# A build-time scheduler that books a port shared by VectorE and GpSimd, with costs taken from a trace: hybrid decoder trunk, 2 layers, 1 core

## The chip, the cores and the metric

The kernel runs on one core of a Trainium2 chip. The time is the device time of one execution in microseconds (us). An execution under the profiler gives the traces; its own time is listed beside its span.

The engines are called as the profile calls them: PE (TensorE, with PEld for its weight loads), DVE (VectorE), ACT (ScalarE), POOL (GpSimd) and SP (SyncE, whose queue issues the DMAs). SBUF is the on-chip memory, PSUM the accumulators that PE writes.

## The reference

Two layers over x of 512 tokens by 1024 channels, all in float32. Each layer is a mixer and a feed-forward part, with an RMS norm ahead of each and one behind it, added to x. In short:

```
for l in range(2):
    h = rmsnorm(x, pre_mix_norm[l])
    proj = h @ w_in[l]                    # k, v, q, z: 4 heads of 128; bq, bk, bv: 8 heads of 64; a, b
    q, k, v = silu(causal_conv4(q, k, v)) # q, k then l2-normalised
    o_a = gated_delta_rule(q, k, v, g, beta)      # chunked; triangular solve in each chunk
    o_a = rmsnorm(o_a, dn_out_norm) * silu(z)
    o_b = dilated_attention(rope(bq), rope(bk), bv)   # three window/dilation pairs
    x = x + rmsnorm(concat(o_a, o_b) @ w_out[l], post_mix_norm[l])
    h = rmsnorm(x, pre_ffn_norm[l])
    u = causal_conv3(h @ ffn_up[l]) + bias
    x = x + rmsnorm((gelu(gate) * val) @ ffn_down[l], post_ffn_norm[l])
```

## The kernel before, in words

Channels lie on the 128 partitions and the 512 tokens along a row, so x is 8 tiles of 128x512. A float32 product with a weight is made of three products in the type fp32r: the high part of the weight with the high and with the low part of x, and the low part of the weight with the high part of x (`mm3`, L305; `mmk`, L310). Each weight comes in units of 128x1024. `loader` issues the DMA of a unit into one of two `raw` buffers. `splitter` has ACT copy it to fp32r (`whi`), then subtracts that from `raw` to get `wlo`: VectorE in one operation of 128x1024, or GpSimd in four of 128x256. Four pairs of buffers (`HL`) hold split units; a new copy to `whi` waits until PE has finished the unit that had the buffer before.

The order of every engine's instructions is made at build time by a small scheduler, `_Sched` (L46). It has a clock `t`, which each matmul moves on (`mm`, L132), and for VectorE, ACT and GpSimd a time from which each is free. The parts of the computation are generators (`gates`, `decays`, `conv`, `silu`, `inverse`, `attention`, `score`, `splitter` and so on). Each emits instructions, books their cost with `op` (L76) and yields until the time at which it may go on; the job with the best priority whose time has come goes next. So a changed cost changes no instruction's work, but can change the order of emission, and that is the program's order on each engine. It can also change which engine does a step where the scheduler may choose: the `wlo` split (VectorE or GpSimd), and the scaling of an attention row by its reciprocal sum (ACT or GpSimd, `score`). On the chip each engine then runs its list in order and waits for what it needs.

What the change's steps touch, in the mixer:

- The units come in the order k, v (4 heads each), bq, bk, bv (4 units each), q, z, then 8 of the out-projection. The convolution of k and v (`conv`, L779) is `A<-psg,rs` on VectorE, one step on ACT and three on VectorE (`kT<-A,vv,kT`, 128x509 to 128x511; `vb<-A,vv,vb` for v).
- `gates` (L712) works out the decay gate `dn_g` on VectorE in small steps, and then has PE multiply it with a triangle: `pso<-dn_g,cc`. `silu` (L803) of k loads ACT's silu table, runs kT (128x2048) and loads the exp table again.
- `decays` (L765): four times `pso<-cc,dn_g` on PE, `edec<-pso,dn_gc` on VectorE (L771), two steps on ACT. PSUM tag `o` has one buffer, so the next product waits for the `edec` before it.
- `k_head` (L819): transposes of kT (`pss<-cc,kT`), a square and its sum, and `kd<-pss,dn_kds`; tag `s` has three buffers.
- `inverse` (L860) solves the triangles, with two round trips through DRAM, and `attention` (L1180) makes 8 heads of 4 scores: `psg<-bT,..` on PE, the masked minimum `nm` on VectorE, exp and its sum `den` on ACT, a reciprocal on VectorE, the scaling of `A` or `B` on ACT or GpSimd, transposes on PE (`psg<-cc,B`), a copy `pt` on ACT and its low part on VectorE, and the product with `vh`. The last of it and z (`zt`) become `hx`, which the out-projection multiplies.

The cost lines before the change, for VectorE's and GpSimd's two-operand step (`tt`):

```
n = out_.free_size()
return sc.op(eng, 0.07 + n * 1.05e-3 if eng == "dve" else 0.18 + n * 2.07e-3, after)
```

Of the kernel before, what the change touches and what calls it, by code (L numbers as in the profile page):

```python
# [43 lines left out]
class _Sched:  # L44
# [69 lines left out]
def kernel(ctx: ExitStack, tc: tile.TileContext, xT, w_ab, w_cm, w_tm, w_o, w_up, w_dn,  # L114
# [14 lines left out]
    sc = _Sched()  # L129


    def mm(ps, lhsT, rhs, start, stop):  # L132
        n = rhs.free_size()
        if rhs.dtype == F32R:
            sc.t += n / 2400.0 if n >= 256 else 0.107
        else:
            sc.t += max(0.214 if lhsT.free_size() > 64 else 0.11, n / 600.0)
        pe.matmul(ps, lhsT, rhs, start=start, stop=stop)  # L138

    def transposes(dst, srcs):  # L140
        for i, s in enumerate(srcs):
            sc.t += 0.109
            pe.transpose(dst[:, i * P:(i + 1) * P], s, ident)

# [5 lines left out]
    def tt(out_, a, b, op, after=0.0, eng="dve"):  # L150
        (nc.vector if eng == "dve" else nc.gpsimd).tensor_tensor(out_, a, b, op=op)  # L151
        n = out_.free_size()
        return sc.op(eng, 0.07 + n * 1.05e-3 if eng == "dve" else 0.18 + n * 2.07e-3, after)

    def ts(out_, a, s1, s2, op0, op1=None, after=0.0, eng="dve"):
        e = nc.vector if eng == "dve" else nc.gpsimd
        if op1 is None:
            e.tensor_scalar(out_, a, s1, None, op0=op0)  # L158
# [3 lines left out]
        return sc.op(eng, 0.07 + n * 1.0e-3 if eng == "dve" else 0.17 + n * 8.5e-4, after)

    def stt(out_, a, s, b, op0, op1, after=0.0):
        nc.vector.scalar_tensor_tensor(out_, a, s, b, op0=op0, op1=op1)  # L165
        return sc.op("dve", 0.07 + out_.free_size() * 1.05e-3, after)
# [1394 lines left out]
```

## Time and profile before

| what | value |
|---|---|
| median of 3 runs | 1411.7 us (1410.64 to 1413.77) |
| profiled execution: its time | 1419.57 us |
| profiled execution: its span | 1417.5 us |
| mean granted PE clock | 0.981 |
| matmuls on PE in the profile | 7174 |
| table loads on ACT | 19, 24.4 us in all |

A row of the page gives an engine's busy time, its share of the span and its count. A row of the windows gives a stretch, its length, then busy time and count of PE, PEld, DVE, ACT and POOL, the granted clock, the DMA share and GB/s. A row of the timeline gives the start, the length, the engine, the kernel's line, the operation, out<-in, the shape and how many in a row, and in brackets the idle time of the engine ahead of it with what ended it; rows of one kind in a row are drawn together. Float32 matmuls stand in the records as two each, so x8 is four products.

### The profile page before, as it was taken

What the parts mean: (1) busy time and instruction counts of PE and PEld (TensorE: products, weight loads), DVE (VectorE), ACT (ScalarE), POOL (GpSimd) and SP (SyncE); (2) the same over time, 40 slices, a digit from 0 to 9 for tenths busy, and PEclk for the clock granted to TensorE, in tenths of its full rate; (3) what the DMA queues carried; (4) which work ended last, traced back from release to release, by engine and by line L of the source; (5) the groups of instructions that cost most, each with busy time, mean ns of one, the idle gap of its engine ahead of it and who ended that gap; (6) DMA issues with size and microseconds to landing.
All of it is one profiled execution on the core that took longest, in us unless ns stands there. A gap on an engine that the chain in (4) does not pass through costs nothing. (4 is left out here: it accounts for less than half of the span.)

```text
span 1417.5 us, 19282 instructions
## 1 busy us (share of the span) xinstructions
PE 1375.4 (97%) x7174; PEld 1145.6 (81%) x7174; DVE 861.9 (61%) x1512; ACT 618.0 (44%) x998; POOL 719.2 (51%) x778
## 2 busy tenths in 40 slices
PE   9999999998999999999989999999989999999996
PEld 5878777887888888888878887788888888888886
DVE  4774477847677777421569544778478777773213
ACT  5553466635544344232345433665345444433220
POOL 5455266414577777334173541663155777772441
PEclk9999999999999999999999987999999999999998
DMA  5233111052233232333332330110512333333331
GB/s 200 75 94 87 61 46 45 16 164 75 72 92 104 90 105 89 94 98 99 98 131 68 116 88 16 45 46 23 171 60 79 100 97 98 94 96 88 106 93 60
DMA packets 48701, 123.17 MB, mean 87 GB/s; under 512 B 15584, under 2 KB 18400, under 8 KB 48608
## 3 DMA queue, kind: packets, MB, share of 16 engines
q1 hardware_dynamic: 48608, 121.95, 27.8%
q8 instruction: 57, 0.93, 0.3%
q14 instruction: 36, 0.29, 0.1%
HBM read 115.11 MB, written 6.82 MB: 86 GB/s over the span
## 5 line engine op out<-in xcount | busy, mean ns | idle before, releaser
L151 POOL TENSOR_TENSOR wlo<-raw,whi 128x256 fp32r<-128x256 f32 x560 | 500.8, 925 | 357.9 <-ACT whi L147 343.9
L138 PE MATMUL psg<-hx,whi 128*128 128x512 f32 (+1 forms) x2080 | 631.9, 387 | 2.4 <-DVE hx L151 2.4
L138 PEld LDWEIGHTS psg<-hx,whi 128*128 128x128 f32 x2080 | 379.9, 189 | 76.1 <-DVE hx L151 3.4
L138 PE MATMUL psg<-hx,wlo 128*128 128x512 f32 (+1 forms) x1040 | 396.5, 381 | 0.0
L147 ACT ACTIVATE whi<-raw 128x1024 fp32r<-128x1024 f32 (+1 forms) x200 | 209.0, 1045 | 428.1 <-PE psg L138 367.5
L138 PEld LDWEIGHTS psg<-hx,wlo 128*128 128x128 f32 x1040 | 196.3, 189 | 38.2
L165 DVE SCALAR_TENSOR_TENSOR B<-A,vv,B 128x510 f32<-128x510 f32 (+1 forms) x176 | 199.4, 1135 | 39.3 <-ACT B L147 36.1
L138 PE MATMUL psg<-hid,whi 128*128 128x512 f32 (+1 forms) x744 | 213.1, 371 | 0.0
L138 PEld LDWEIGHTS psg<-hid,whi 128*128 128x128 f32 x744 | 135.6, 188 | 24.1
L151 DVE TENSOR_TENSOR wlo<-raw,whi 128x1024 fp32r<-128x1024 f32 (+1 forms) x58 | 73.7, 1273 | 133.6 <-ACT whi L147 133.6
L138 PE MATMUL psg<-hid,wlo 128*128 128x512 f32 (+1 forms) x372 | 137.9, 371 | 0.0
L138 PE MATMUL psg<-whi,hx 128*128 128x512 f32 x384 | 125.0, 407 | 0.7 <-DVE A L151 0.7
L151 POOL TENSOR_TENSOR acc<-acc,sq 128x256 f32<-128x256 f32 (+1 forms) x65 | 65.8, 1013 | 104.4 <-ACT sq L147 102.5
L151 DVE TENSOR_TENSOR A<-psg,rs 128x512 f32<-128x512 f32 x100 | 68.7, 689 | 40.8 <-PE psg L138 38.8
L138 PEld LDWEIGHTS psg<-whi,hx 128*128 128x128 f32 x384 | 70.1, 191 | 14.6 <-DVE A L151 1.5
L138 PEld LDWEIGHTS psg<-hid,wlo 128*128 128x128 f32 x372 | 70.0, 188 | 12.0
L138 PE MATMUL psg<-wlo,hx 128*128 128x512 f32 x192 | 76.2, 397 | 0.0
L147 ACT ACTIVATE B<-A,vv 128x512 f32<-128x512 f32 x88 | 70.2, 802 | 2.6 <-DVE A L151 2.6
L147 ACT ACTIVATE C<-B 128x512 f32<-128x512 f32 x44 | 27.7, 630 | 86.2 <-DVE B L165 86.1
L151 DVE TENSOR_TENSOR hid<-C,hid 128x512 fp32r<-128x512 f32 x44 | 36.3, 826 | 28.3 <-ACT hid L147 28.3
L158 POOL TENSOR_SCALAR B<-B,den 128x512 f32<-128x512 f32 (+1 forms) x30 | 41.0, 1368 | 23.8 <-DVE den L177 13.7
L138 PE MATMUL pss<-hx,whome 128*128 128x256 f32 x288 | 42.6, 305 | 5.2 <-DVE hx L165 4.6
(239 smaller groups left out, 1704.8 us busy)
## 6 DMA issues: line engine op xcount, KB each, us to landing
raw<-in_w_up_dram SPq DMA_DIRECT2D x88, 512.0 KB, 3.5
raw<-in_w_cm_dram SPq DMA_DIRECT2D x32, 512.0 KB, 3.6
raw<-in_w_dn_dram SPq DMA_DIRECT2D x32, 512.0 KB, 3.5
raw<-in_w_tm_dram SPq DMA_DIRECT2D x24, 512.0 KB, 3.5
raw<-in_w_o_dram SPq DMA_DIRECT2D x16, 512.0 KB, 3.5
raw<-in_w_dn_dram SPq DMA_DIRECT2D x16, 384.0 KB, 3.1
xt<-in_xT_dram SPq DMA_DIRECT2D x7, 512.0 KB, 7.0
scr_a<-am SPq DMA_DIRECT2D x8, 256.0 KB, 2.7
```

The source lines that it names most:

```text
L138: pe.matmul(ps, lhsT, rhs, start=start, stop=stop)
L147: nc.scalar.activation(out_, in_, func, **kw)
L151: (nc.vector if eng == "dve" else nc.gpsimd).tensor_tensor(out_, a, b, op=op)
L158: e.tensor_scalar(out_, a, s1, None, op0=op0)
L165: nc.vector.scalar_tensor_tensor(out_, a, s, b, op0=op0, op1=op1)
```

## The change

`_Sched` gets a time `port` from which the way to SBUF that VectorE and GpSimd share is free. An operation booked with `port=True` starts no earlier than that and moves it to its own end. VectorE's `tt`, `ts` and `stt` book it unless an operand lies in PSUM (`in_psum`); GpSimd's always do. The costs of these steps and the pitch of the products change: a product of n columns in fp32r from n/2400 to n/2400 + 0.0134, GpSimd's `ts` from 0.17 + n x 8.5e-4 to 0.17 + n x 2.7e-3, and so on. `tiled` moves the clock on by 0.095 whenever the stationary tile goes between up to 64 and more rows or columns. The same matmuls are made, and the same buffers are used; what changes is the order on each engine and the engine of some steps.

```
--- before.py
+++ after.py
@@ -55,6 +55,7 @@
         self.slots = {}
         self.flags = {}
         self.chain = False
+        self.port = 0.0
 
     def spawn(self, gen, prio=1, at=0.0):
         self.jobs.append([prio, self.n, max(self.t, at), gen])
@@ -73,8 +74,12 @@
             except StopIteration:
                 self.jobs.remove(job)
 
-    def op(self, eng, cost, after=0.0):
+    def op(self, eng, cost, after=0.0, port=False):
+
         start = max(self.free[eng], self.t, after)
+        if port:
+            start = max(start, self.port)
+            self.port = start + cost
         self.free[eng] = start + cost
         return start + cost + 0.2
 
@@ -129,16 +134,29 @@
     sc = _Sched()
 
 
+    shape = [None]
+
+    def tiled(lhsT):
+        now = (lhsT.shape[0] <= 64, lhsT.free_size() <= 64)
+        if now != shape[0]:
+            shape[0] = now
+            sc.t += 0.095
+
     def mm(ps, lhsT, rhs, start, stop):
         n = rhs.free_size()
+        tiled(lhsT)
         if rhs.dtype == F32R:
-            sc.t += n / 2400.0 if n >= 256 else 0.107
+            sc.t += n / 2400.0 + 0.0134 if n >= 256 else 0.107
         else:
-            sc.t += max(0.214 if lhsT.free_size() > 64 else 0.11, n / 600.0)
+            sc.t += max(0.22 if lhsT.free_size() > 64 else 0.117, n / 600.0 + 0.01)
         pe.matmul(ps, lhsT, rhs, start=start, stop=stop)
+
+    def in_psum(*aps):
+        return any(a.tensor.name.startswith("ps") for a in aps)
 
     def transposes(dst, srcs):
         for i, s in enumerate(srcs):
+            tiled(s)
             sc.t += 0.109
             pe.transpose(dst[:, i * P:(i + 1) * P], s, ident)
 
@@ -150,7 +168,9 @@
     def tt(out_, a, b, op, after=0.0, eng="dve"):
         (nc.vector if eng == "dve" else nc.gpsimd).tensor_tensor(out_, a, b, op=op)
         n = out_.free_size()
-        return sc.op(eng, 0.07 + n * 1.05e-3 if eng == "dve" else 0.18 + n * 2.07e-3, after)
+        if eng == "dve":
+            return sc.op(eng, 0.09 + n * 1.06e-3, after, not in_psum(a, b))
+        return sc.op(eng, 0.18 + n * 2.2e-3, after, True)
 
     def ts(out_, a, s1, s2, op0, op1=None, after=0.0, eng="dve"):
         e = nc.vector if eng == "dve" else nc.gpsimd
@@ -159,11 +179,13 @@
         else:
             e.tensor_scalar(out_, a, s1, s2, op0=op0, op1=op1)
         n = out_.free_size()
-        return sc.op(eng, 0.07 + n * 1.0e-3 if eng == "dve" else 0.17 + n * 8.5e-4, after)
+        if eng == "dve":
+            return sc.op(eng, 0.09 + n * 1.05e-3, after, not in_psum(a))
+        return sc.op(eng, 0.17 + n * 2.7e-3, after, True)
 
     def stt(out_, a, s, b, op0, op1, after=0.0):
         nc.vector.scalar_tensor_tensor(out_, a, s, b, op0=op0, op1=op1)
-        return sc.op("dve", 0.07 + out_.free_size() * 1.05e-3, after)
+        return sc.op("dve", 0.09 + out_.free_size() * 1.13e-3, after, not in_psum(a, b))
 
     def red(out_, a, after=0.0):
         nc.vector.tensor_reduce(out_, a, axis=AX.X, op=ALU.add)
```

Where the program differs, at the two places that the prediction speaks of. Names carry a tile's number, which differs between the kernels; lines of the kernel after are 18 to 22 higher.

The first place is layer 0, where the decays start. PE before: the second and the third decay product (`pso<-cc,dn_g`), with three of kT's four transposes between them. Fifteen fp32r products follow the third one, the first six in these rows, and then the fourth.

```order
L138 MATMUL pso_582<-cc_80,dn_g_305 128x128 x4
L143 MATMUL pss_587<-cc_80,kT_292 128x128 x4
L143 MATMUL pss_595<-cc_80,kT_292 128x128 x4
L143 MATMUL pss_602<-cc_80,kT_292 128x128 x4
L138 MATMUL pso_609<-cc_80,dn_g_305 128x128 x4
L138 MATMUL psg_536<-hx1_105,whi_372 128x512 x2
L138 MATMUL psg_536<-hx1_105,wlo_373 128x512
L138 MATMUL psg_624<-whi_450,hx0_104 128x512 x2
L138 MATMUL psg_624<-wlo_451,hx0_104 128x512
```

PE after, from the first of kT's transposes to the first products of bq behind them:

```order
L161 MATMUL pss_595<-cc_80,kT_289 128x128 x4
L161 MATMUL pss_602<-cc_80,kT_289 128x128 x4
L161 MATMUL pss_611<-cc_80,kT_289 128x128 x4
L152 MATMUL pso_618<-cc_80,dn_g_302 128x128 x4
L152 MATMUL pso_642<-cc_80,dn_g_302 128x128 x4
L161 MATMUL pss_650<-cc_80,kT_289 128x128 x4
L152 MATMUL psg_664<-whi_424,hx0_104 128x512 x2
L152 MATMUL psg_664<-wlo_425,hx0_104 128x512
```

The second decay product (`pso_618`) has moved behind three transposes, and the third (`pso_642`) follows it directly; the fourth transpose of kT comes after both.

VectorE there, before: `edec` of the first three decay products and the six steps of v's convolution.

```order
L151 TENSOR_TENSOR edec_294<-pso_561,dn_gc_309 128x512
L151 TENSOR_TENSOR edec_294<-pso_582,dn_gc_309 128x512
L165 SCALAR_TENSOR_TENSOR vb_293<-A_534,vv_89,vb_293 128x509
L165 SCALAR_TENSOR_TENSOR vb_293<-A_534,vv_89,vb_293 128x510
L165 SCALAR_TENSOR_TENSOR vb_293<-A_534,vv_89,vb_293 128x511
L165 SCALAR_TENSOR_TENSOR vb_293<-A_559,vv_89,vb_293 128x509
L165 SCALAR_TENSOR_TENSOR vb_293<-A_559,vv_89,vb_293 128x510
L165 SCALAR_TENSOR_TENSOR vb_293<-A_559,vv_89,vb_293 128x511
L151 TENSOR_TENSOR edec_294<-pso_609,dn_gc_309 128x512
```

And after:

```order
L169 TENSOR_TENSOR A_568<-psg_420,rs_103 128x512
L169 TENSOR_TENSOR wlo_563<-raw_536,whi_562 128x1024
L169 TENSOR_TENSOR edec_291<-pso_570,dn_gc_306 128x512
L187 SCALAR_TENSOR_TENSOR vb_290<-A_550,vv_89,vb_290 128x509
L187 SCALAR_TENSOR_TENSOR vb_290<-A_550,vv_89,vb_290 128x510
L187 SCALAR_TENSOR_TENSOR vb_290<-A_550,vv_89,vb_290 128x511
L187 SCALAR_TENSOR_TENSOR vb_290<-A_568,vv_89,vb_290 128x509
L187 SCALAR_TENSOR_TENSOR vb_290<-A_568,vv_89,vb_290 128x510
L187 SCALAR_TENSOR_TENSOR vb_290<-A_568,vv_89,vb_290 128x511
L169 TENSOR_TENSOR edec_291<-pso_618,dn_gc_306 128x512
```

`edec` of the second product has moved behind the six steps, and the split of bq's last unit (`wlo_563`), which GpSimd did, stands ahead of the first.

ACT there, before: from the last convolution step of k through silu of kT between its two table loads to the copy of bq's last unit, `whi_628`.

```order
L147 ACTIVATE kT_292<-A_496,vv_89 128x512
L147 ACTIVATE whi_540<-raw_486 128x1024
L219 ACT_TABLE_LOAD
L147 ACTIVATE kT_292<-kT_292 128x2048
L219 ACT_TABLE_LOAD
L147 ACTIVATE vb_293<-A_534,vv_89 128x512
L147 ACTIVATE vb_293<-A_559,vv_89 128x512
L147 ACTIVATE edec_294<-edec_294 128x512 x2
L147 ACTIVATE sq_592<-pss_587 128x512
L147 ACTIVATE sq_600<-pss_595 128x512
L147 ACTIVATE edec_294<-edec_294 128x512 x2
L147 ACTIVATE whi_628<-raw_532 128x1024
```

And after, where that copy is `whi_562`:

```order
L165 ACTIVATE kT_289<-A_502,vv_89 128x512
L165 ACTIVATE whi_547<-raw_525 128x1024
L165 ACTIVATE whi_562<-raw_536 128x1024
L241 ACT_TABLE_LOAD
L165 ACTIVATE kT_289<-kT_289 128x2048
L241 ACT_TABLE_LOAD
L165 ACTIVATE vb_290<-A_550,vv_89 128x512
L165 ACTIVATE vb_290<-A_568,vv_89 128x512
```

The copy has moved from behind the decays' steps to ahead of the silu and its table load.

The second place is the end of attention in layer 0 (layer 1 reads the same). ACT before: `A` and `B` with `den` are exps of scores, the last one `B_2586`; `zt` 128x1536 is silu of three heads of z.

```order
L147 ACTIVATE A_2485,den_2584<-A_2485,nm_2549 128x384
L147 ACTIVATE sq_2592<-vb_293 128x512
L147 ACTIVATE bT0_298<-pso_2519 64x512
L147 ACTIVATE vb_293<-pss_2608,vv_89 128x4x128
L147 ACTIVATE B_2586,den_2617<-B_2586,nm_2589 128x512
L219 ACT_TABLE_LOAD
L147 ACTIVATE pt0_1479<-psg_2625 128x2x128
L147 ACTIVATE pt1h_1480<-psg_2641 128x3x128
L147 ACTIVATE zt_2166<-zt_2166 128x1536
```

And after, where the last exp is `B_2598`:

```order
L165 ACTIVATE pt1h_1305<-psg_2588 128x4x128
L165 ACTIVATE A_2567,den_2596<-A_2567,nm_2570 128x384
L241 ACT_TABLE_LOAD
L165 ACTIVATE zt_2072<-zt_2072 128x1536
L165 ACTIVATE vb_290<-pss_2613,vv_89 128x4x128
L165 ACTIVATE pt0_1304<-psg_2619 128x128
L165 ACTIVATE B_2526<-B_2526,den_2573 128x256
L241 ACT_TABLE_LOAD
L165 ACTIVATE B_2598,den_2624<-B_2598,nm_2601 128x512
L241 ACT_TABLE_LOAD
L165 ACTIVATE bT0_295<-pso_2542 64x512
```

The silu of z with its table load has moved ahead of the last exp, which has a load on both sides now, and a scaling (`B_2526<-B_2526,den`) that GpSimd did has come to ACT.

VectorE there, before, around the last reciprocal (`den_2617`):

```order
L151 TENSOR_TENSOR bT0_298<-pso_2519,bT0_298 64x512
L151 TENSOR_TENSOR zt_2166<-psg_2317,rs_103 128x512
L177 RECIPROCAL den_2617<-den_2617 128x1
L151 TENSOR_TENSOR vb_293<-vb_293,dn_rq_314 128x4x128
L151 TENSOR_TENSOR pt0_1479<-psg_2625,pt0_1479 128x2x128
L151 TENSOR_TENSOR pt1l_1481<-psg_2641,pt1h_1480 128x3x128
L151 TENSOR_TENSOR zt_2166<-zt_2166,vb_293 128x512 x3
L151 TENSOR_TENSOR pt1l_1481<-psg_2672,pt1h_1480 128x4x128
L151 TENSOR_TENSOR zt_2166<-psg_2630,rs_103 128x512
```

And after, around `den_2624`:

```order
L169 TENSOR_TENSOR pt0_1304<-psg_2619,pt0_1304 128x128
L169 TENSOR_TENSOR zt_2072<-zt_2072,vb_290 128x512 x3
L169 TENSOR_TENSOR zt_2072<-psg_2575,rs_103 128x512
L199 RECIPROCAL den_2624<-den_2624 128x1
L169 TENSOR_TENSOR bT0_295<-pso_2542,bT0_295 64x512
L169 TENSOR_TENSOR pt0_1304<-psg_2656,pt0_1304 128x2x128
L169 TENSOR_TENSOR pt1l_1306<-psg_2663,pt1h_1305 128x3x128
L169 TENSOR_TENSOR hx0_2668<-zt_2072,hx0_2668 128x512
```

The product of z with the recurrence's output (`vb`) and the last head's `zt<-psg` have moved ahead of the last reciprocal.

More of the change, by code (lines that the diff above doesn't have):

```diff
@@ L57, in __init__ @@
         self.chain = False
+        self.port = 0.0
     def spawn(self, gen, prio=1, at=0.0):
@@ L74, in run, with op @@
                 self.jobs.remove(job)
-    def op(self, eng, cost, after=0.0):
+    def op(self, eng, cost, after=0.0, port=False):
         start = max(self.free[eng], self.t, after)
+        if port:
+            start = max(start, self.port)
+            self.port = start + cost
         self.free[eng] = start + cost
@@ L129, with tiled, in_psum @@
     sc = _Sched()
+    shape = [None]
+    def tiled(lhsT):
+        now = (lhsT.shape[0] <= 64, lhsT.free_size() <= 64)
+        if now != shape[0]:
+            shape[0] = now
+            sc.t += 0.095
     def mm(ps, lhsT, rhs, start, stop):
         n = rhs.free_size()
+        tiled(lhsT)
         if rhs.dtype == F32R:
-            sc.t += n / 2400.0 if n >= 256 else 0.107
+            sc.t += n / 2400.0 + 0.0134 if n >= 256 else 0.107
         else:
-            sc.t += max(0.214 if lhsT.free_size() > 64 else 0.11, n / 600.0)
+            sc.t += max(0.22 if lhsT.free_size() > 64 else 0.117, n / 600.0 + 0.01)
         pe.matmul(ps, lhsT, rhs, start=start, stop=stop)
+    def in_psum(*aps):
+        return any(a.tensor.name.startswith("ps") for a in aps)
     def transposes(dst, srcs):
         for i, s in enumerate(srcs):
+            tiled(s)
             sc.t += 0.109
@@ L152, in tt @@
         n = out_.free_size()
-        return sc.op(eng, 0.07 + n * 1.05e-3 if eng == "dve" else 0.18 + n * 2.07e-3, after)
+        if eng == "dve":
+            return sc.op(eng, 0.09 + n * 1.06e-3, after, not in_psum(a, b))
+        return sc.op(eng, 0.18 + n * 2.2e-3, after, True)
     def ts(out_, a, s1, s2, op0, op1=None, after=0.0, eng="dve"):
@@ L161, in ts @@
         n = out_.free_size()
[L162 removed]
+        if eng == "dve":
+            return sc.op(eng, 0.09 + n * 1.05e-3, after, not in_psum(a))
+        return sc.op(eng, 0.17 + n * 2.7e-3, after, True)
     def stt(out_, a, s, b, op0, op1, after=0.0):
         nc.vector.scalar_tensor_tensor(out_, a, s, b, op0=op0, op1=op1)
[L166 removed]
+        return sc.op("dve", 0.09 + out_.free_size() * 1.13e-3, after, not in_psum(a, b))
     def red(out_, a, after=0.0):
```

## The prediction

> **What bounds the kernel now.** I read the page first, then the windows, the waits of TensorE (PE) and the timelines of the places that wait. The first block is the page; the second is busy time by stretch (PE, PEld, DVE, ACT, POOL, granted clock, DMA share).
>
> ```profile
> span 1417.5 us, 19282 instructions
> PE 1375.4 (97%) x7174; PEld 1145.6 (81%) x7174; DVE 861.9 (61%) x1512; ACT 618.0 (44%) x998; POOL 719.2 (51%) x778
> ```
> ```profile
> 70.00:105.00 35.00, 32.89 (x179) 27.15 (x178) 27.92 (x67) 20.26 (x27) 19.79 (x26) 1.00 0.32 95
> 735.00:770.00 35.00, 32.84 (x162) 27.35 (x162) 30.27 (x53) 20.20 (x31) 16.04 (x20) 0.95 0.25 81
> 1085.00:1400.00 315.00, 315.00 (x1444) 263.08 (x1443) 169.45 (x175) 113.16 (x144) 180.00 (x191) 1.00 0.30 91
> ```
> ```profile
> 143.18:176.05 32.87, 32.81 (x268) 25.55 (x268) 15.66 (x59) 14.52 (x33) 8.84 (x11) 1.00 0.18 62
> 839.14:882.44 43.30, 43.08 (x268) 33.80 (x268) 16.16 (x59) 14.53 (x33) 8.81 (x11) 0.72 0.15 49
> ```
>
> PE is the bound. In the feed-forward stretch (1085 to 1400) it is busy without a gap, and the order gives the weight splits there to the same engines as before, so nothing is won or lost there. What can change lies in the two mixers (layer 0 up to about 280, layer 1 from 735 to 985) and the hand-overs between stages. In two of their stretches, 70:105 and 735:770, VectorE is busy for 28 and 30 of 35 us and PE has gaps: what VectorE is given there, PE feels. The last two rows are the same 268 matmuls in layer 0 and layer 1: 10.4 us more at a clock of 0.72. The profiled execution took 1419.57 us (span 1417.5 and 2.1 around it), 7.9 above the median of 1411.7; I put that down to such stretches and add my sum to the median, clock left out. This kernel's runs tell about 0.2% (2.8 us) from no change.
>
> The waits of PE (total, times, longest):
>
> ```profile
> PE psg L138 <- DVE hx L151: 2.4, 2, 1.2
> PE pso L138 <- DVE dn_g L165: 1.9, 1, 1.9
> PE pss L143 <- DVE A L151: 1.9, 4, 0.5
> PE psg L138 <- DVE nm L1208: 1.7, 2, 0.9
> ```
>
> In the mixers all are small, 8 us together. A new order can win at most these, and it loses wherever it puts a dependent product nearer to its source than the chain on the other engines is long. So I went through the order of both kernels for the places where that distance changes.
>
> **Layer 0, the decays: the largest term.** The four decay products `pso<-cc,dn_g` share one PSUM buffer, so each waits for VectorE's `edec` of the one before. Before, in PE, ACT and DVE:
>
> ```profile
> 60.58 1.05 PE L138 MATMUL pso<-cc,dn_g 128*128 128x128 f32 x8
> ...
> 62.86 0.62 PE L138 MATMUL psg<-hx,whi 128*128 128x512 f32 x2
> ...
> 63.55 1.05 PE L138 MATMUL pso<-cc,dn_g 128*128 128x128 f32 x8
> 64.44 1.47 PE L143 MATMUL pss<-cc,kT 128*128 128x128 f32 x12
> 65.75 1.06 PE L138 MATMUL pso<-cc,dn_g 128*128 128x128 f32 x8
> 66.56 0.70 PE L138 MATMUL psg<-hx,whi 128*128 128x512 f32 x2
> ...
> 70.83 1.16 PE L138 MATMUL pso<-cc,dn_g 128*128 128x128 f32 x8 [0.58 <-DVE edec L151]
> ...
> 75.24 0.74 PE L138 MATMUL psg<-whi,hx 128*128 128x512 f32 x2 [0.33 <-DVE A L151]
> ```
> ```profile
> 61.63 1.92 ACT L147 ACTIVATE kT<-kT 128x2048 f32<-128x2048 f32 x1 [1.30 <-DVE kT L165]
> 63.57 1.28 ACT L219 ACT_TABLE_LOAD   x1
> 64.86 1.33 ACT L147 ACTIVATE vb<-A,vv 128x512 f32<-128x512 f32 x2
> ...
> 69.45 1.04 ACT L147 ACTIVATE whi<-raw 128x1024 fp32r<-128x1024 f32 x1
> ```
> ```profile
> 65.62 4.55 DVE L165 SCALAR_TENSOR_TENSOR vb<-A,vv,vb 128x509 f32<-128x509 f32 x6 [0.29 <-ACT vb L147]
> 70.09 0.69 DVE L151 TENSOR_TENSOR edec<-pso,dn_gc 128x512 f32<-128x512 f32 x1
> ...
> 71.92 0.68 DVE L151 TENSOR_TENSOR kd<-pss,dn_kds 128x512 f32<-128x512 f32 x1
> ...
> 75.11 0.68 DVE L151 TENSOR_TENSOR edec<-pso,dn_gc 128x512 f32<-128x512 f32 x1
> ```
>
> A group of three fp32r products takes 0.69 (62.86 to 63.55), one 0.23. The new order does three things. First, 12 more of them stand ahead of the gates' product, and as many as before between it and the decays, so the first decay product moves to 60.58 + 12 x 0.23 = 63.34; nothing else is late by then. Second, ACT copies bq's last weight unit (`whi_562`) ahead of the silu of kT; that copy needs the buffer of the last v unit, which PE finishes only at 63.3 (before, this copy stood behind: the row at 69.45). So ACT: copy to 64.4, table load to 65.7, silu 1.92 to 67.6, load to 68.9, convolution of v from 68.9. VectorE's six steps start 0.76 behind (64.86 to 65.62): 69.7. Third, `edec` of the second product now stands behind these six, and the third product follows the second on PE with nothing between. `edec` starts 4.47 after the six start (65.62 to 70.09): 74.15, done 74.85. PE is there at 63.34 + 0.81 (a decay product, 65.75 to 66.56) + 2.76 (12 products) + 1.31 (kT's transposes, 64.44 to 65.75) + 0.81 = 69.0, and waits 5.9; before, it waited 0.58 once. Queued behind the waiting copy on ACT are the two loads, the silu and all of v's convolutions; VectorE's split of the same unit waits too (64.4 to 65.7), and the first `edec` behind it is done by 66.4, before PE needs it at 68.2. GpSimd waits for nothing there. Behind it, kd ends 1.82 after `edec` (70.78 to 72.60): 76.7; from there one reduction, kd, two A and `edec` make 3.2 (72.60 to 75.79 before, same five and a 0.2): done 79.9; the fourth product ends at 80.8. The same work was behind PE at 75.24 before: **+5.55**. Below: were the copy out of the silu's way, silu would start when VectorE's kT steps end. That was 61.6; a split moved onto VectorE ahead of them adds 1.27, and as POOL stands aside for it about 0.7 goes:
>
> ```profile
> L151 DVE TENSOR_TENSOR wlo<-raw,whi 128x1024 fp32r<-128x1024 f32 (+1 forms) x58 | 73.7, 1273 | 133.6 <-ACT whi L147 133.6
> ```
>
> So 62.2, 3.5 earlier, +2.05. Above: a half-clock stretch behind so long a wait, +1.7 more (3.41 us at half). I take 5.55: every link stands in the order.
>
> **Layer 1, gates and decays.**
>
> ```profile
> 744.63 0.59 PE L138 MATMUL pso<-dn_g,cc 128*128 128x16 f32 x4 [1.91 <-DVE dn_g L165]
> ```
> ```profile
> 757.38 1.92 ACT L147 ACTIVATE kT<-kT 128x2048 f32<-128x2048 f32 x1
> ```
> ```profile
> 750.37 6.11 DVE L165 SCALAR_TENSOR_TENSOR kT<-A,vv,kT 128x509 f32<-128x509 f32 x6
> ...
> 765.83 0.69 DVE L151 TENSOR_TENSOR edec<-pso,dn_gc 128x512 f32<-128x512 f32 x1
> ```
> ```profile
> 751.35 4.57 POOL L151 TENSOR_TENSOR wlo<-raw,whi 128x256 fp32r<-128x256 f32 x4 [7.60 <-ACT whi L147]
> ```
> ```profile
> 70.57 2.80 POOL L151 TENSOR_TENSOR wlo<-raw,whi 128x256 fp32r<-128x256 f32 x4 [7.72 <-ACT whi L147]
> ```
>
> The 12 products more (2.76) cover the 1.91 wait: PE has the gates' product at 742.72 + 2.76 = 745.5. But the fourth decay product now comes 3 products after the third, where it came 21 after. PE is at it at 745.5 + 0.44 + 48 x 0.23 + 0.81 + 9 x 0.23 + 0.81 + 1.31 + 0.81 + 3 x 0.23 = 763.5 (0.44 for the gates' product, the others as above). It needs the third `edec`, which ended at 766.52. VectorE is quicker by 1.56 where POOL's split beside its six kT steps goes (6.11 against 4.55) and pays 1.27 for doing that split itself, so the kT steps end at 756.2; silu, which a load held until 757.38, can start 1.2 earlier, and `edec` ends at 765.3. The wait is 1.9, as long as the one removed: **0**. Below, -2.0 (the chain 2 earlier still); above, +1.2 (silu held as before).
>
> In these rows VectorE's six operations and POOL's four take 4.55 and 2.80 apart, 7.35 one after the other; side by side all ten are done in 6.1. They slow each other, but less than if each waited for the other's end, so the new booking makes VectorE later than it is. That is how a copy that isn't ready comes to stand ahead of a silu that is.
>
> On this the Trainium skill says, page "SBUF — State Buffer", section "Who interferes with whom": the port pair that VectorE and GpSimd share is an exclusive lock for a whole instruction, and the other engine fully blocks. That is how the change books it.
>
> **End of attention, each layer.**
>
> ```profile
> 269.70 2.09 POOL L158 TENSOR_SCALAR B<-B,den 128x512 f32<-128x512 f32 x1
> ```
> ```profile
> 275.65 0.38 PE L138 MATMUL pso<-pt1l,vh 128*128 128x256 f32 x1 [0.27 <-DVE pt1l L151]
> ...
> 278.16 0.50 PE L138 MATMUL psg<-hx,whi 128*128 128x512 f32 x1 [1.19 <-DVE hx L151]
> ```
>
> Before, the last score's exp, its scaling (2.09 on POOL) and its transposes were through before PE came; the waits were 0.27 and 1.19. Now ACT runs an exp, load, silu of z, load, the last exp, load, where it ran both exps and then one load and the silu; and VectorE takes `zt<-psg` ahead of the last reciprocal. That needs the last z product, after which PE has only 0.82 of work (seven small matmuls, an estimate) to the transposes. 0.69 (`zt`, as `edec` at 70.09, which reads PSUM too) + 0.15 (the reciprocal, an estimate) + 2.09 and three hand-overs of 0.05 less 0.82 is a wait of 2.25; the out-projection's `hx` is ready behind it. 2.25 less 0.27 and 1.19, two layers: **+1.6**. Below, -0.5 (the scaling half as long); above, +4.2 (the last exp one load of 1.28 later than that in each layer).
>
> The row of the load at 63.57 (1.28) ends at 64.85, and the next operation starts at 64.86. The Trainium skill, page "ScalarE: Activation LUTs", section "What ACT_TABLE_LOAD costs", states 1.28 and a drain of 1.38 with each switch, which speaks against this change: with two drains more in each layer's chain this term could be 5.5 larger. No drain shows in this row.
>
> **Array changes.** Counted in both orders, PE changes its tile size 124 times instead of 108.
>
> ```profile
> 162.67 0.62 PE L138 MATMUL psg<-hx,whi 128*128 128x512 f32 x2
> 163.13 0.40 PE L138 MATMUL psg<-hx,wlo 128*128 128x512 f32 x1
> 163.46 0.65 PE L138 MATMUL pss<-C,xiT 128*64 128x32 f32 x8
> ```
>
> 0.33 against 0.23 where the tile stays: 0.10 x 16 = **+1.6**, 0 if under idle time.
>
> **Smaller gains.** Rope's transposes have 12 products more ahead of them; half of the 1.9 of A: **-1.0** (0 to -1.9). Attention now starts ahead of the inverse's steps and runs among them, so its scores have more products around them; half of nm's 1.7: **-0.85** (0 to -1.7). With the inverse its round trips through DRAM move on SP's queue; PE has attention's products ahead meanwhile, and the weights' loads wait for their own buffers: 0. The 20 scalings that change between POOL and ACT are only paid where they end a chain, as above. The hand-overs between stages keep their products within 15 of where they were: 0, 3 either way.
>
> Sum: 5.55 + 0 + 1.6 + 1.6 - 1.0 - 0.85 = **+6.9**: 1418.6. The profiled execution would stand at 1426.5 if its clock stretches stayed.
>
> **Rivals.** *Faster, 0.14:* VectorE, rid of POOL's splits beside its kT and v steps, has layer 0's `edec` done when PE comes, and ACT's copy finds its buffer free because PE reached the last v unit sooner. The point from which it decides is an `edec` done by 69.0. Then layer 0 costs 0, layer 1's gates keep 2.0, rope and nm give all of 3.6, the end of attention 0.5, and the array changes cost 1.6: -4.5, **1407.2**. For it: the six kT steps beside POOL show 1.56 to win. Against it: silu, a load and six steps (1.92 + 1.28 + 4.55) don't fit between 62.2 and 69.0.
>
> *No change, 0.18:* the block costs its lower bound of 2.05 and the gates keep 2.0; with 1.6 + 1.6 - 1.85 from the rest that is +1.4, **1413.1**. For it: the copy needs only to be 3.5 earlier. Against it: the order puts it ahead of the silu, and its buffer is PE's to free.
>
> *The booking is right, 0.06:* if VectorE's operations wait out POOL's, its kT steps end as late as the scheduler has them, and the copy delays nothing: 2.05 for 5.55 gives 6.9 - 3.5, **1415.1**. This is what follows from the lock of the Trainium skill's page "SBUF — State Buffer". Against it stand the 6.1 for 7.35 above.
>
> **How the numbers follow.** The forecast has 0.62, by itself 1414.6 to 1426: low with 3 less at the hand-overs and 1 less at the block, high with 1.7 of half clock, 2.6 at attention's end and 3 at the hand-overs more. The range of 1408 to 1426 takes in these three cases but the ends; it leaves out most of the faster case and a tail above, about 2 in 10. Slower: 0.62 + the lock's share 0.04 = 0.66; same: 0.18 + 0.02 = 0.20; faster 0.14.
>
> **What would show it.** Layer 0's third decay product with a wait of 4 to 6 us on edec, silu of kT started near 65.7 behind a whi; no wait on dn_g in layer 1 but one of 2 on edec; two waits near 2.2 on POOL's or ACT's B in PE's transposes, 23 table loads. It is wrong if the edec waits stay under 1 us, or if the inverse's stretch in layer 1 decides through the clock.

## The result, and the profile after

| kernel | median of its runs | runs | ratio to before, 95% interval |
|---|---|---|---|
| before | 1412.24 us (1410.64 to 1413.77) | 4 | |
| changed | 1430.39 us (1429.22 to 1431.12) | 4 | 1.0117 (1.009 to 1.0145) |

The change makes the kernel 18 us slower by the medians (16.5 us by the ratio), where 6.9 was forecast. The profiled execution of the changed kernel took 1431.12 us, its span is 1429.3. The kernel before had been profiled in an execution with a half-clock stretch of its own (842 to 866 us, where the granted clock was 0.50) and a mean clock below that of most of its runs, so I compare with a second profile of it, of a run of 1410.38 us (e1 below). The head of the page, of the kernel before (second profile) and then of the changed one:

```profile
span 1408.2 us, 19282 instructions
PE 1365.3 (97%) x7174; PEld 1137.8 (81%) x7174; DVE 861.2 (61%) x1512; ACT 618.0 (44%) x998; POOL 720.5 (51%) x778
```
```profile
span 1429.3 us, 19268 instructions
PE 1375.5 (96%) x7174; PEld 1151.8 (81%) x7174; DVE 828.6 (58%) x1517; ACT 629.5 (44%) x1014; POOL 675.8 (47%) x744
```

The same 7174 matmuls keep PE busy 10.2 us longer, and PE is idle 10.9 us longer (53.8 against 42.9): two parts, of which the forecast had priced one. VectorE and GpSimd both work less than before, and still PE waits more.

PE's waits after (total, times, longest; the helper `mm` is L152 here and L138 before):

```profile
PE pso L152 <- DVE edec L169: 7.7, 2, 4.8
PE pso L152 <- DVE acc L169: 6.8, 5, 2.0
PE pso L152 <- ACT pt1h L165: 6.1, 2, 3.0
PE pso L152 <- POOL rtp L387: 5.6, 5, 1.8
...
PE psg L152 <- DVE zt L169: 4.1, 2, 2.1
```

Before, no wait in the mixers was over 1.9. The waits on `acc` and `rtp` belong to the hand-overs between stages, and the second profile of before has them too:

```profile
PE pso L138 <- DVE acc L151: 4.4, 4, 2.2
PE pso L138 <- POOL rtp L365: 4.2, 4, 1.5
```

The windows after, of the stretches quoted before and, below, of the wait on `zt` and of what follows it (the columns are those of the windows before):

```profile
70.00:105.00 35.00, 29.74 (x163) 25.74 (x161) 29.71 (x60) 19.14 (x26) 11.06 (x13) 0.90 0.18 61
735.00:770.00 35.00, 32.93 (x165) 27.20 (x163) 25.20 (x47) 12.61 (x22) 18.11 (x19) 1.00 0.48 160
1085.00:1400.00 315.00, 315.00 (x1395) 260.99 (x1394) 161.44 (x184) 119.77 (x153) 185.49 (x201) 1.00 0.31 94
```
```profile
228.00:231.00 3.00, 0.95 (x5) 0.78 (x5) 2.96 (x5) 2.97 (x4) 3.00 (x4) 0.99 0.00 0
231.00:234.40 3.40, 3.40 (x14) 3.01 (x13) 1.53 (x6) 3.35 (x5) 1.67 (x2) 0.51 0.53 153
```

The feed-forward part is as it was. In the last row PE has no gap, but runs at a clock of 0.51. The changed kernel's profile has 15 such stretches of 3.41 us inside its work; the second profile of before has 6. Of the nine more, four stand at the decays, two behind the wait on `zt`, three in the inverse (at 172.9, 876.0 and 879.5 us) and one in a hand-over, and the one behind layer 1's wait on `dn_g` is gone. Ahead of the inverse's, PE is idle for only 0.29 and 0.66 us of a window, so those three are not explained by a wait.

The start of the nth matmul, same n in all profiles, shows where time is lost, in us. The column before is the second profile of before, the others what comes on top (runs e3, e9 and e10 are described below):

| n | place | before | changed | e3 no booking | e9 booking at decays | e10 booking elsewhere |
|---|---|---|---|---|---|---|
| 226 | layer 0, ahead of the decays | 58.9 | +1.7 | +0.4 | +1.5 | -0.6 |
| 405 | behind the decays | 92.1 | +7.5 | +2.9 | +7.2 | +1.9 |
| 2100 | feed-forward | 388.1 | +11.8 | +1.7 | +9.3 | +6.5 |
| 3830 | layer 1, behind the gates | 752.0 | +7.3 | -0.5 | +4.4 | +4.7 |
| 3990 | behind the decays | 783.1 | +14.3 | +2.1 | +11.0 | +8.2 |
| 5700 | feed-forward | 1076.7 | +21.4 | +4.0 | +14.0 | +15.2 |

The places of the prediction, in the changed kernel. PE at layer 0's decays, then ACT there, then VectorE:

```profile
64.46 1.05 PE L152 MATMUL pso<-cc,dn_g 128*128 128x128 f32 x8
...
70.27 1.06 PE L152 MATMUL pso<-cc,dn_g 128*128 128x128 f32 x8
76.14 2.07 PE L152 MATMUL pso<-cc,dn_g 128*128 128x128 f32 x8 [4.80 <-DVE edec L169]
```
```profile
64.57 1.06 ACT L165 ACTIVATE whi<-raw 128x1024 fp32r<-128x1024 f32 x1 [4.38 <-PE psg L152]
65.65 1.28 ACT L241 ACT_TABLE_LOAD   x1
66.94 1.91 ACT L165 ACTIVATE kT<-kT 128x2048 f32<-128x2048 f32 x1
```
```profile
66.81 0.68 DVE L169 TENSOR_TENSOR edec<-pso,dn_gc 128x512 f32<-128x512 f32 x1
70.92 4.56 DVE L187 SCALAR_TENSOR_TENSOR vb<-A,vv,vb 128x509 f32<-128x509 f32 x6 [3.44 <-ACT vb L165]
75.40 0.68 DVE L169 TENSOR_TENSOR edec<-pso,dn_gc 128x512 f32<-128x512 f32 x1
```

ACT waits 4.38 for the buffer of the copy, the silu starts at 66.94, VectorE stands idle for 3.44, and PE then waits 4.80: the chain of the prediction, link by link. The third product takes 2.07 instead of 1.05: it runs at half clock.

Layer 1's decays and the end of attention in layer 0, PE:

```profile
779.09 1.16 PE L152 MATMUL pso<-cc,dn_g 128*128 128x128 f32 x8 [2.94 <-DVE edec L169]
```
```profile
287.65 0.80 PE L152 MATMUL pso<-pt,vh 128*128 128x256 f32 x4 [3.05 <-ACT pt1h L165]
```

### The profile page after: what moved, and what is told of

The parts are those of the page before. It is cut to its first block, busy times and chain, and to the rows that moved or that the text cites. A ratio compares the mean times of both kernels' runs of the same rounds, so it can differ in the third digit from the quotient of the medians.

```text
span 1429.3 us, 19268 instructions
## 1 busy us (share of the span) xinstructions
PE 1375.5 (96%) x7174; PEld 1151.8 (81%) x7174; DVE 828.6 (58%) x1517; ACT 629.5 (44%) x1014; POOL 675.8 (47%) x744
## 4 chain that ended last, share of the span: by engine, by line
PE 84%; DVE 9%; ACT 3%; DMA 2%; issue 1%; POOL 1%; SPq 0%; ACTq 0%; DVEq 0%; POOLq 0%
PE psg L152 71%; PE pss L152 7%; PE pso L152 2%; DMA raw<-in_w_up_dram 2%; DVE hx L187 2%; PE pss L161 1%; PE psg L161 1%; DVE xt L169 1%; DVE wlo L169 1%; DVE kT L187 1%; ACT L241 1%; DVE vb L187 1%; DVE A L169 1%; ACT whi L165 1%; DVE C L169 0%
## 5 line engine op out<-in xcount | busy, mean ns | idle before, releaser
L152 PE MATMUL psg<-hx,whi 128*128 128x512 f32 (+1 forms) x2080 | 638.0, 390 | 4.1 <-DVE zt L169 4.1
L169 POOL TENSOR_TENSOR wlo<-raw,whi 128x256 fp32r<-128x256 f32 x530 | 462.6, 904 | 336.3 <-ACT whi L165 336.3
L152 PEld LDWEIGHTS psg<-hx,whi 128*128 128x128 f32 x2080 | 385.3, 191 | 82.4 <-DVE zt L169 5.8
L152 PE MATMUL psg<-hx,wlo 128*128 128x512 f32 (+1 forms) x1040 | 398.8, 383 | 0.0
L152 PEld LDWEIGHTS psg<-hx,wlo 128*128 128x128 f32 x1040 | 198.3, 191 | 37.9
L152 PE MATMUL psg<-hid,whi 128*128 128x512 f32 (+1 forms) x744 | 213.4, 371 | 0.0
L187 DVE SCALAR_TENSOR_TENSOR B<-A,vv,B 128x510 f32<-128x510 f32 (+1 forms) x176 | 184.5, 1062 | 17.6 <-ACT B L165 14.4
L152 PEld LDWEIGHTS psg<-hid,whi 128*128 128x128 f32 x744 | 135.7, 188 | 24.1
L169 DVE TENSOR_TENSOR wlo<-raw,whi 128x1024 fp32r<-128x1024 f32 (+1 forms) x65 | 83.3, 1286 | 104.5 <-ACT whi L165 104.4
L152 PE MATMUL psg<-hid,wlo 128*128 128x512 f32 (+1 forms) x372 | 137.9, 371 | 0.0
L152 PE MATMUL psg<-whi,hx 128*128 128x512 f32 x384 | 122.8, 401 | 2.1 <-DVE A L169 2.1
L152 PEld LDWEIGHTS psg<-whi,hx 128*128 128x128 f32 x384 | 71.5, 192 | 16.7 <-DVE A L169 2.1
L152 PEld LDWEIGHTS psg<-hid,wlo 128*128 128x128 f32 x372 | 70.1, 188 | 12.0
L152 PE MATMUL psg<-wlo,hx 128*128 128x512 f32 x192 | 75.8, 395 | 0.0
L169 DVE TENSOR_TENSOR A<-psg,rs 128x512 f32<-128x512 f32 x100 | 65.3, 681 | 5.7 <-PE psg L161 5.6
L178 POOL TENSOR_SCALAR A<-A,den 128x384 f32<-128x384 f32 (+1 forms) x30 | 29.5, 984 | 74.4 <-ACT xw L165 31.5
L152 PEld LDWEIGHTS psg<-wlo,hx 128*128 128x128 f32 x192 | 36.6, 191 | 7.9
L152 PE MATMUL pss<-hx,whi 128*128 128x256 f32 (+1 forms) x144 | 36.6, 337 | 4.7 <-DVE hx L187 3.6
```

## The experiments

My theory after the result: each wait costs its length, and where it is long a stretch at half clock besides, so that the clock, which I had left out, is half of the loss. The rivals: the waits alone, with a clock that goes its own way; the table loads; the new durations rather than the booking. Each ratio below is to runs of the kernel before on the same chip, made together with the run; not all runs were on one chip, so small differences between them are read from the ratios.

**e1: before again.**

> The kernel before, unchanged, for the granted clock of its timed runs. Waits-and-clock theory (each new wait of PE costs its length and, where it is long, a half-speed stretch behind it): about 1412 us, and a mean clock of about 0.985 in the timed runs, above the 0.981 of the profiled execution shown, whose 26 us at clock 0.72 around 840 to 865 us (10 us more in PE's own time) would then be absent. Waits-alone rival (the clock follows the chip and not the kernel, and is the same for both): 0.978 to 0.981 as in the changed kernel's runs, and the whole loss is direct waits.

1413.74 us (10 runs, 1410.00 to 1425.85), ratio 1.0014 (0.9989 to 1.0039). The clock was 0.985 to 0.989 in eight runs, and 0.981 and 0.977 in the two slowest (1421.19 and 1425.85). The changed kernel's four runs had 0.978 to 0.980. So runs with a lower clock come now and then, as the first profile of before was one (0.981, with its long stretch), and the changed kernel is below before's usual clock in all its runs. The Trainium skill, page "TensorE: Matmul & The Clock Gate", section "What's actually happening", has a clock that is full or half, decided in windows of 3413 ns that run freely; the traces agree, every half-clock stretch that ends inside the work is a multiple of 3.41 us.

**e3, e4, e8: which part of the change.** e3 leaves out the booking (`if port:` never holds), e4 keeps only the booking, e8 books less of each operation:

```
e3: -        if port:
    +        if False:
e4: the cost lines, the pitch and tiled() as in the kernel before
e8: -            self.port = start + cost
    +            self.port = start + 0.81 * cost
```

> The changed kernel without the booking of the shared way to memory; the new durations, pitches and array changes stay. If the booking makes the loss: 1412 to 1416 us, with 19 table loads and no copy ahead of the silu of kT. If the new durations make it: 1425 to 1430 us. My forecast's terms give 1412.2 + 1.6 for the array changes + 0.5 to 2 for the end of attention = 1414 to 1416 us.

> The kernel before with the booking alone: old durations, old pitch, no array changes booked. The order has 25 table loads and layer 0's decays spaced as before. If the booking makes the loss through the whole kernel: 1430.4 less the layer-0 decays' 6 to 9 us = 1421 to 1425 us. If booking and durations are only bad together (the booking with GpSimd's too short scaling costs is harmless): 1411 to 1415 us. If the table loads themselves cost: above 1430 us.

> The changed kernel, except that each booking holds the shared way for 0.81 of the operation's length. 0.81 is from the traces: with both engines busy, VectorE's three-tap step takes 1.22 us against 0.75 alone and GpSimd's split 1.18 against 0.74, so that 1.22 us do the work of 1.51. If a full lock is merely too long: most of the 17 us come back, 1413 to 1420 us. If any booking moves the products to places where their sources aren't ready: 1425 us or more, and waits of 2 us and over stay at other places.

| run | median | ratio, 95% interval | table loads |
|---|---|---|---|
| e3 no booking | 1413.25 | 1.0010 (0.9995 to 1.0025) | 19 |
| e4 booking alone | 1453.48 | 1.0287 (1.0267 to 1.0308) | 25 |
| e8 booking of 0.81 | 1429.90 | 1.0116 (1.0099 to 1.0133) | 23 |

The booking makes the loss; the durations, the pitch and the array changes without it do nothing that can be measured. e4 came out above 1430, where only the rival of the table loads had it; but that rival is not shown by it, since all else moved too (waits of 2.1 in nm's place, 2.9 on a row factor, 3.8 on edec), and e7 below loses 4 loads of 23 and no time. What e4 does show is that the booking with GpSimd's old, too short scaling costs is far worse than with the new ones. And a booking of 0.81 of each length is no better: at 0.81 the two largest waits of e8 are 4.1 on edec, and others of 2.06 stand at places where the changed kernel has none.

**e9, e10: where.** A flag switches the booking on only from a mixer's start to its last decay (e9), or only outside (e10).

```
-        if port:
+        if port and self.on:
```

> The changed kernel with the booking switched on only from a mixer's start to its last decay, in both layers; behind that the order is nearly that of the kernel without booking (19 table loads), and the decays' products stand as in the changed kernel. By stages of the traces, the changed kernel against the one without booking: 4.6 us at layer 0's decays and 4.4 at layer 1's. Additive theory: 1413.3 + 9 = 1422 us (1419 to 1425). Rival, that later waits on VectorE swallow most of an early delay (undoing the copy's place moved layer 0's decays by 2.3 us and the whole by 1): 1414 to 1418 us.

> The other half: booking off from a mixer's start to its last decay, on everywhere else. The order is the changed kernel's but for the decays, which stand as in the kernel before. Additive theory: 1430.4 - 9 = 1421 us (1418 to 1424). Rival, that later waits swallow an early delay: 1426 to 1430 us.

e9: 1423.96, ratio 1.0083 (1.0069 to 1.0097). e10: 1426.76, ratio 1.0105 (1.0092 to 1.0118). e9 is as the additive theory had it. e10 is where its rival had it. Against e3's 1.0010 each half alone costs 0.73% and 0.95%, both together 1.07%: of 10.3 + 13.4 = 23.7 us, 8.6 are counted twice. Part of that is no saving: with the booking off behind the decays e9's order there still isn't e3's, and from n 405 to 2100 it falls 2.1 us further behind before, where e3 catches up 1.2. In layer 0 itself the delay of the decays isn't swallowed: the changed kernel is 5.6 us behind e10 at n 405 and 5.3 at n 2100.

**e2, e13, e14: the wait on edec.**

```
e2:  in splitter, unit 11 of layer 0:  +  yield from sc.wait((0, "ksilu"))   # set behind the silu of kT
e13: in conv, v's heads 0 and 1, ahead of the three steps:  +  yield from sc.wait(K("third"))
e14: in decays, ahead of the third product:  +  yield sc.t + 4.5
```

> The changed kernel, except that the weight copy that now stands ahead of the silu of kT in layer 0 is made to wait for it, so that the decays' products there are spaced as before. Waits-and-clock theory: the delay of 5.8 us at the layer-0 decays goes, and the half-speed stretches behind the two waits there with it: 1430.4 - 5.8 - 1.7 to 3.4 = 1421 to 1423 us. Waits-alone rival: 1424.6 us, mean clock unchanged. A third one, that the delay there comes from the splits that the port booking sends to VectorE and not from the copy's place: 1429 to 1431 us, and a wait of 4 to 5 us on edec is still there.

> The changed kernel, except that the six three-tap steps of v's first two heads are issued behind the decays' third subtraction on VectorE. If they are what the third product's wait of 4.8 us on edec ends on: that wait falls below 1 us and the delay at the end of layer 0's decays from 7.5 us against the kernel before to 2 to 4; the whole 1425 to 1427 us. Rival, that VectorE's work bounds the stretch whatever its order: the wait comes back as one of 3 to 5 us on A, whose buffers v's steps then hold, the delay stays at 6 to 8 us and the whole at 1429 to 1431 us.

> The changed kernel, except that the decays' third product is issued 4.5 us later in the scheduler's clock, so that other products can stand ahead of it, as in the kernel before. If the loss is that PE has nothing queued while VectorE gets to the second subtraction: the wait on edec falls below 1.5 us, the delay at the end of layer 0's decays to 2 to 4 us, the whole 1425 to 1427 us. If VectorE bounds the stretch: the wait moves to A, the whole 1429 to 1431 us.

e2: 1429.34, ratio 1.0115 (1.0093 to 1.0137). e13: 1436.75, 1.0150 (1.0105 to 1.0195). e14: 1430.63, 1.0097 (1.0064 to 1.0130). PE in e2, e13 and e14, and behind them VectorE in e2:

```profile
66.24 1.05 PE L152 MATMUL pso<-cc,dn_g 128*128 128x128 f32 x8
68.44 1.06 PE L152 MATMUL pso<-cc,dn_g 128*128 128x128 f32 x8
74.29 2.07 PE L152 MATMUL pso<-cc,dn_g 128*128 128x128 f32 x8 [4.10 <-DVE edec L169]
```
```profile
74.17 1.16 PE L152 MATMUL pso<-cc,dn_g 128*128 128x128 f32 x8 [1.27 <-DVE edec L169]
82.61 1.22 PE L152 MATMUL psg<-whi,hx 128*128 128x512 f32 x2 [7.28 <-DVE A L169]
```
```profile
77.42 1.09 PE L161 MATMUL pss<-cc,kT 128*128 128x128 f32 x4 [6.28 <-DVE kd L169]
```
```profile
67.33 0.69 DVE L169 TENSOR_TENSOR edec<-pso,dn_gc 128x512 f32<-128x512 f32 x1 [2.27 <-PE pso L152]
67.93 5.70 DVE L187 SCALAR_TENSOR_TENSOR vb<-A,vv,vb 128x509 f32<-128x509 f32 x6
```

In e2 the silu starts at 61.99, near the 61.11 of before, and the loss behind the decays shrinks only from 5.8 to 4.7 (the rows of n 226 and 405: 0.5 and 5.2 in e2). The copy's place is a fifth of it. In e2 PE has run 12 products more ahead of the decays and has one group of three left ahead of the fourth decay product, the row with the wait; in the second profile of before five groups stand there, and the wait is 0.60. VectorE's second `edec` has itself waited 2.27 for PE, and its six steps of v take 5.70 beside a split of GpSimd's, where they took 4.55. The time and the wait of e2 are what its third rival had, but not for the cause that it gave: VectorE does no split between 57 and 74 us. In e13 the wait on edec falls to 1.27 and in e14 it goes, and a longer one stands at a later product (7.28 on A, 6.28 on kd): PE's other work needs buffers that the same VectorE steps free. What is lost when VectorE is starved (3.44 us idle here) is paid at one product or the next. At n 405 e13 and e14 are 10.2 and 10.8 behind before, more than either of their theories had (2 to 4, or 6 to 8 for e13), and e13 as a whole is above the ranges of both. So the rival of e13 and e14 holds only in that no order tried gets the loss back; that VectorE's work fills the stretch is not so, as it is idle in it.

**e7, e15: the wait at the attention's end.** e7 has z's silus wait for the last exp, which takes the table loads out from between; e15 also puts z's three gating steps behind the sum `bT<-pso,bT` that frees the one output buffer.

```
e7:  -            if heads[0]:
     +            if kind == "z":
e15: e7, and in z_head:  +  wait for K("bt", AH - 2), set behind the head's sum
```

> The changed kernel, except that z's silus wait until the last exponential of the attention has been issued: 19 table loads in place of 23, and none between the attention's last exponentials and copies. Waits-and-clock theory: the wait of 3.05 us at the attention's end falls by one load of 1.28 us and the split behind it in both layers, and a half-speed stretch of 1.6 us with it: 1425 to 1427 us. If ACT's part of it is covered by VectorE's queue: 1429 to 1431 us.

> The changed kernel with z's silus behind the last exponential, as in the earlier run, and z's three gating steps on VectorE behind the sum that frees the attention's only output buffer. If that buffer's release is what the wait of 3.05 us at the attention's end ends on, with the table load or the gating steps ahead of it: the wait falls to 1.0 to 1.5 us in both layers, and the whole to 1425 to 1427 us. If the hand-over behind it is paced by z's gated rows anyway: its waits grow by as much, and the whole stays at 1429 to 1431 us.

e7: 1430.13, ratio 1.0118 (1.0103 to 1.0133); e15: 1430.33, 1.0100 (1.0064 to 1.0136). ACT in the changed kernel, VectorE and then PE in e7, PE in e15:

```profile
284.90 1.28 ACT L241 ACT_TABLE_LOAD   x1
286.20 0.59 ACT L165 ACTIVATE bT<-pso 64x512 f32<-64x512 f32 x1
```
```profile
283.08 1.89 DVE L169 TENSOR_TENSOR zt<-zt,vb 128x512 f32<-128x512 f32 x3 [2.64 <-ACT zt L165]
284.90 0.68 DVE L169 TENSOR_TENSOR zt<-psg,rs 128x512 f32<-128x512 f32 x1
285.50 0.67 DVE L169 TENSOR_TENSOR bT<-pso,bT 64x512 f32<-64x512 f32 x1
```
```profile
286.32 0.97 PE L152 MATMUL pso<-pt,vh 128*128 128x256 f32 x4 [3.06 <-DVE bT L169]
```
```profile
285.99 0.36 PE L152 MATMUL pso<-pt,vh 128*128 128x256 f32 x1 [1.27 <-ACT pt1h L165]
288.04 0.56 PE L152 MATMUL pso<-pt,vh 128*128 128x256 f32 x3 [1.69 <-DVE pt L169]
```

Three causes stand in a row. First the copy of the output buffer comes behind a table load; without the load the sum comes behind the gating steps, and PE waits 3.06 as before; without both the buffer is free 1.8 us sooner, and PE waits 1.27 for it and then 1.69 for the row's probabilities, 2.96 in all. So taking the table loads out of the chain saved nothing here, since what comes next is as late.

**e5, e11: is it the clock?** Products of the identity with itself, unread, on PE's queue ahead of products that wait; e11 keeps only those ahead of the wait on `zt`.

```
+    def fill(ps, n):
+        for _ in range(n):
+            pe.matmul(ps, ident, ident, start=True, stop=True)
...
+                    if name == "z" and h == 1:
...
+                        fill(psum("s")[:, :P], 7)
```

> The changed kernel with idle-time products: 32 products of the identity with itself per layer, whose result nobody reads, put on PE's queue just ahead of five products that wait (7 at 0.22 us ahead of the wait on zt, 9 ahead of the last head's first product with the probabilities, 7, 3 and 6 ahead of the hand-over's sums and row factors); all else stands in the same order. Waits-and-clock theory: the waits still end when they did, but the half-speed stretches behind them go, 7 of the 15 in the changed kernel's profile at about 1.6 us each: 1430.4 - 11 = 1419 us (1417 to 1423), mean clock 0.985 or more. Waits-alone rival (the clock doesn't follow the waits): 1430 to 1433 us, clock 0.978 to 0.980.

> The changed kernel with 7 idle-time products of 0.22 us ahead of the wait on zt alone, in both layers (the wait is 2.05 us, so they lie inside it). Waits-and-clock theory: the half-speed stretch behind that wait goes in both layers and nothing else changes, 1430.4 - 3.2 = 1427 us. Waits-alone rival: 1430.4 us, 1.5 us more if the wait isn't there to hide them.

e11: 1427.34 us (1424.36 to 1429.58), ratio 1.0109 (1.0095 to 1.0122): 3 us less by the medians, as forecast, but by the ratios only 0.0008, 1.1 us, and the intervals overlap, so the saved time isn't shown. What the windows show is the clock; they answer to the two rows above:

```profile
228.00:231.00 3.00, 2.51 (x18) 2.03 (x17) 2.94 (x4) 2.97 (x5) 2.72 (x3) 1.00 0.00 0
231.00:234.40 3.40, 3.40 (x24) 3.00 (x23) 1.56 (x6) 3.35 (x5) 2.13 (x3) 1.00 0.39 110
```

VectorE's and ACT's rows are the same, the wait ends as before, and with PE kept busy in it the clock stays at 1.00: 24 products in the 3.4 us behind, where there were 14. The same holds in layer 1 (0.55 behind the wait on `zt` in the changed kernel, 1.00 in e11).

e5: 1429.51, ratio 1.0111 (1.0094 to 1.0128), with a clock of 0.983 to 0.989 and 7 half-clock stretches in its profile for 15. The clock came back and most of the time didn't: my expectation fell. Its row at the attention's end, PE:

```profile
284.27 2.27 PE L159 MATMUL pso<-cc 128*128 128x128 f32 x18 [2.96 <-DVE bT L173]
```

Nine of the extra products were written to the very buffer that PE waits for, so they stood behind the wait and made it 2 us longer, in both layers. And in the hand-over the sums came sooner, but the wait for `acc` in its second half grew from 0.93 to 2.07, because VectorE's chain ends when it ends. A half-clock stretch ahead of such a wait was free here.

**e6, e12: the same on the kernel before.**

> The kernel before with the same kind of products ahead of its own longer waits: per layer 4 ahead of the output rows' first product, in layer 0 also 5 and 8 in the hand-over, in layer 1 also 6 ahead of the gates' product. Waits-and-clock theory: the half-speed stretches at 278, 329 to 336 and 745 us of its profile go, 4 at 1.6 us: 1412.9 - 6 = 1407 us, faster than both kernels. Waits-alone rival: 1413 to 1415 us, since the extra products can only lengthen what they stand ahead of.

> The kernel before with the earlier idle-time products and 8 more in layer 1, ahead of the wait of 2.04 us for the up-projection's first right-hand side, behind which its profile shows 6.8 us at half the clock. Waits-and-clock theory: 1 to 3 us below the 0.9983 of the run with the earlier ones, a ratio of 0.996 to 0.9975. If VectorE's chain sets the pace there anyway: 0.998 to 0.999.

e6: 1410.96, ratio 0.9983 (0.9967 to 0.9999); e12: 1409.97, ratio 0.9978 (0.9964 to 0.9992). Both are 2 to 3 us below the kernel before, under half of the 6 that I expected of e6, and what e12 gains on e6 is less than the runs can tell. In e6's profile the stretches at 278, 329 to 336 and 745 us are gone, as intended, while one has come in the inverse (842.1) and a second at 1029.9. In e12 the two at 1024.7 and 1028.1, which its 8 products were to remove, are still there: the wait shrank from 2.04 to 0.97, but PE was still idle for 1.26 us of the window ahead. e12 is the fastest kernel here; inside its work its profile has 4 half-clock stretches.

## Why the prediction was off

The direction held, the size didn't: +6.9 forecast, +18.2 measured, past the upper end of 1426. By the two profiles the loss is 10.9 us of idle time and 10.2 us of busy time; the forecast had terms for waits and none for the clock.

- **Layer 0's decays, +5.55.** +5.8 measured between n 226 and 405, with a wait of 4.80 where 5.9 was forecast. The order of events is as written. That the size is so near is partly luck: 4.2 of the 5.8 are idle time and 1.6 are PE at half clock, which I had left out. And the copy's place isn't what makes it: without the copy I had the term at 2.05, e2 shows 4.7.
- **Layer 1, 0.** The wait on dn_g went as forecast, and the half-clock stretch behind it too: from +10.8 at n 3800, ahead of it, to +7.3 at n 3830. The wait on edec was 2.94 (1.9 forecast), waits on A and kd behind it grew from 0.5 to 2.6, and with two stretches the decays cost +7.0. Net +3.5, of which 3.2 is idle time.
- **End of attention, +1.6.** 3.05 in each layer, where I had 2.25, and less 0.27 and 1.19 that makes 3.2: inside its bounds of -0.5 to 4.2. The cause I gave, the scaling on GpSimd behind the last reciprocal, was wrong: e7 and e15 show the output buffer, behind a load or z's gating.
- **Not seen at all:** the wait of 2.05 on `zt` in both layers, where a product needs an accumulator that a z head still holds. With its stretch it is 3.6 a layer. The wait isn't the booking's alone: e3 has it at up to 1.7, without a stretch behind.
- **Clock, 0: the step that failed.** I read the one long stretch of before's profile as chance and so left the clock out of the sum. That stretch comes and goes (e1); the others aren't chance. The new order has nine more of them, up to 1.7 each, and the page shows 10.2 us more of busy PE for the same matmuls. e11 shows that idle PE is the cause for two of them, behind `zt`, and e6 removes four at waits of the kernel before. Three of the nine are in the inverse, behind almost no idle time, and their cause stays open. Not all of the 10.2 would be had back: e5 shows stretches that a later wait swallows.
- **Rope -1.0 and nm -0.85:** the waits on A in rope (1.9) are gone, more than forecast. nm's are 1.1, against 1.7 in the first profile of before but 1.2 in the second, so no gain is shown there.
- **Hand-overs, 0.** The waits on `acc` and `rtp` grew by 3.8 us, and those on VectorE's `hx` ahead of the next part fell by 3.5 (8.0 to 4.5): together inside the 3 either way.
- **Array changes, +1.6:** nothing here isolates them.
- **"The booking is right", 0.06,** fell: e3, without it, is as quick as before, and e8's softer one is no better. Why a softer booking doesn't help stays open beyond its rows; a rule by which a booking would order better wasn't tried.

## What to carry to other kernels

Price a new wait of the bounding engine at its length and, where it leaves PE idle for about 2 us of a 3.41-us window, 1.6 us more, unless a wait that another engine sets follows soon. Before crediting the removal of a wait, look for what is late next: here a table load, a queue position and an operand were each "the" cause of the same 3 us. A scheduler that is told of a real contention can still order worse, as here with the whole of each length and with 0.81 of it; test the order, not the model's truth.

## What the hardware showed that I had not expected

How much idle time in a 3.41-us window brings half clock in the next, counted over the 17 profiles of this study (windows that begin at full clock, without the first and the last stretch):

| PE idle in the window | windows | followed by half clock |
|---|---|---|
| under 1.2 us | 6520 | 19, all with the inverse's small products in the window |
| 1.2 to 1.6 | 57 | 13 |
| 1.6 to 2.0 | 44 | 33 |
| 2.0 and over | 63 | 63 |

The Trainium skill's page "TensorE: Matmul & The Clock Gate", section "What's actually happening", asks for a whole idle window; here 2 us of idle time in a window were always enough, and 1.6 to 2.0 us in 33 of 44. As the windows run freely, the same wait can be split between two: layer 1's 3.05 at the attention's end left 1.50 and 1.55 in two windows and had no stretch behind it, layer 0's left 0.94 and 2.11 and had one.

And the shared way to memory is not locked for the whole length of a step: in e1's trace VectorE's step of 128x510 takes 0.75 with GpSimd idle and 1.22 with GpSimd busy throughout, a quarter of GpSimd's split 0.74 and, beside such steps, 1.18, so that both together do in 1.22 what would take 1.51 in turn. Whether it is locked for a part of each step or divided stays open. VectorE's steps that read PSUM take 0.68 to 0.69 either way. The Trainium skill's page "SBUF — State Buffer", section "Who interferes with whom", has it as an exclusive lock for a whole instruction; these numbers differ, and they decide.
